# Sums of squares on TensorE and single-tile weight folds at the start of a hybrid encoder block

## The chip, the cores and the metric

The kernel runs on one core of a Trainium2 chip. The metric is the device time of one execution in microseconds, median of the runs. The engines named below are TensorE (PE, with its weight loads as PEld), VectorE (DVE), ScalarE (ACT), GpSimd (POOL) and SyncE (SP), whose queue issues most DMAs.

## The reference

One layer over x of 2048 positions and 1024 channels, all in float32.

```python
u = rms_norm(x, norm_in_g)                     # x * rsqrt(mean(x*x) + 1e-6) * g
proj = einsum('bsd,de->bse', u, w_in)          # 1024 -> 4096
pool_x, pool_z, m_x, m_z = split(proj, 4)      # 1024 columns each
y_pool = pool_mixer(pool_x, pool_w, pool_scale) * silu(pool_z)   # windows 2, 4, 8, 16; 256x256 per group
y_m = mlstm_branch(m_x, ...) * silu(m_z)       # 4 heads of 256, both directions, chunks of 128
h = x + einsum('bse,ed->bsd', concat(y_pool, y_m), w_out)
return rms_norm(h, norm_out_g)
```

## The kernel before

The input projection is done in two halves of 1024 positions. A half is held as 16 tiles `xs[t, kt]` of 128 channels by 512 positions (t: which 512 positions, kt: which 128 of the 1024 channels). The projection's columns are taken in 16 units of 256, and each unit is one step of Strassen's scheme: seven products P1 to P7 instead of eight, each of 12 matmuls with 512 columns (three per channel block: both operands are split into a high part in fp32r and the rest, `bh`, `bl`, `ah`, `al`). One product is one slot: slots 0 to 6 are the first unit, in the order P1, P2, P5, P6, P7, P3, P4, and slot 7 is P1 of the second unit.

PE, DVE, ACT and POOL run in the order in which the program writes their instructions (a hand-written schedule); DMAs on SP are outside that order. Work that is not part of a product is tied to slots by `at_slot(slot, where, ...)`: "pre" stands ahead of the product, "end" behind it. A slot runs like this: `begin_a` (POOL, sums of weights for the slot four later), `read_banks` (ACT or DVE empty the banks of the product before), `low_a` and `high_a` (weight splits for slots ahead), the "pre" events, the product, the "end" events.

The start of the first half has two side tasks, and the change concerns both.

The norm. `squares(t, kt)` squares a tile on ACT, and DVE adds it to `rn[t]`. `norm_sums` adds over the 128 channels with four one-column matmuls (`rhs=ones[:, 0:1]`), DVE scales, POOL takes the power -1/2. `norm_spread` puts the factors across the partitions with four matmuls against the identity, and ACT copies them to `rn[t]`. Then `scale_x` scales each tile on DVE, `sum_b` forms a product's differences on DVE, `high_b` casts four tiles on ACT, and `low_b` subtracts on DVE. While PE waits, `busy(8)` gives it matmuls whose result nobody reads, and 28 such warm-up matmuls (`warm`) stand at the very start. The second half's norm, much later, uses the same `squares` and `norm_sums`; that stays.

The fold. `pool_w` is multiplied into the first quarter of `w_in`: 16 pieces of two tiles, a tile being two float32 matmuls of 256 columns (each is two instructions on PE) into a PSUM buffer `hw` of a pool of three, a copy on ACT (L295) into one of three buffers `st`, and a DMA to `wp_s`. `fold()` is a generator; `fold_steps(n)` takes n steps of it. Loads go out three pieces ahead. Float32 matmuls show as two instructions each, so the four matmuls of `norm_sums` are eight.

Of the kernel before, what the change touches and what calls it, by code (L numbers as in the profile page):

```python
# [10 lines left out]
F32 = mybir.dt.float32  # L11
F32R = mybir.dt.float32r
AF = mybir.ActivationFunctionType
ALU = mybir.AluOpType
# [3 lines left out]
P = 128  # L18
S = 2048
D = 1024  # L20
KT = D // P
NB = 4
BT = S // NB
# [4 lines left out]
EPS = 1e-6  # L28
# [25 lines left out]
def hymba_block(ctx, tc, xT, x, w_in, wpxT, pool_w, bqT, bkT, bvT, bv, w_g, b_g, par, edge, w_out, g_out, out):  # L54
    nc = tc.nc

    def open_pool(stack, name, bufs=1, side="left", **kw):
        return stack.enter_context(tc.tile_pool(name=name, bufs=bufs, side=side, reuse_waits="tile", **kw))
# [4 lines left out]
    wp_s = dram.tile([8, P, KT, P], F32, name="wp_s")  # L63
# [14 lines left out]
    ones = cpool.tile([P, P], F32, name="ones")  # L78
# [10 lines left out]
    ob = open_pool(ctx, "ob", bufs=4)  # L89
# [23 lines left out]
    psp = open_pool(ph1, "psp", side="right", space=PSUM)  # L113
    bstack = {k: ExitStack() for k in reversed(PRODUCTS)}
    bpool = {k: open_pool(stack, f"b{k}", side="right") for k, stack in bstack.items()}
    B, A, raw, sums = {}, {}, {}, {}
# [78 lines left out]
    xs, rn, rs, xq = {}, {}, {}, {}  # L195

    def load_x(pool, p, t):
        for kt in range(KT):
            xs[t, kt] = pool.tile([P, BT], F32, name=f"x{t}{kt}")
            nc.sync.dma_start(out=xs[t, kt], in_=xT[2 * p + t][:, kt, :])  # L200

    def squares(t, kt):
        sq = ob.tile([P, BT], F32, name="op")
        nc.scalar.activation(sq, xs[t, kt], AF.Square)
        if kt == 0:
            rn[t] = xq[t].tile([P, BT], F32, name=f"rn{t}")
            nc.vector.tensor_copy(rn[t], sq)
        else:
            nc.vector.tensor_tensor(rn[t], rn[t], sq, op=ALU.add)

    def norm_sums(pool, t):
        ss = psg.tile([P, 512], F32, name="pg")
        for i in range(4):
            nc.tensor.matmul(ss[:, i:i + 1], lhsT=rn[t][:, i * P:(i + 1) * P], rhs=ones[:, 0:1], start=True, stop=True)
        rs[t] = pool.tile([P, 4], F32, name=f"rs{t}")
        nc.vector.tensor_scalar(rs[t], ss[:, 0:4], 1.0 / D, EPS, op0=ALU.mult, op1=ALU.add)
        nc.gpsimd.tensor_tensor(rs[t], rs[t], mhalf, op=ALU.pow)

    def norm_spread(t):
        rb = psg.tile([P, BT], F32, name="pg")  # L220
        for i in range(4):
            nc.tensor.matmul(rb[:, i * P:(i + 1) * P], lhsT=rs[t][:, i:i + 1].to_broadcast([P, P]), rhs=ident,
                             start=True, stop=True)
        nc.scalar.copy(rn[t], rb)

    def scale_x(t, kt):
        nc.vector.scalar_tensor_tensor(xs[t, kt], in0=xs[t, kt], scalar=par_sb[:, kt, 9:10], in1=rn[t], op0=ALU.mult,
                                       op1=ALU.mult)
# [18 lines left out]
    def low_b(k):  # L247
        hi, lo = B[k]
        for q in range(4):
            nc.vector.tensor_tensor(lo[:, q], block(k, q), hi[:, q].bitcast(F32), op=ALU.subtract)  # L250
# [8 lines left out]
    def unit(U):  # L259
        return PLANS[U // UNITS][U % UNITS]  # L260
# [4 lines left out]
    psk = open_pool(pmp, "psk", bufs=3, space=PSUM)  # L265
# [4 lines left out]
    AHEAD = 3  # L270

    def fold():
        pws, wts = {}, {}
        pieces = [(g, kt) for g in range(4) for kt in range(0, KT, 2)]

        def load(g, kt):
            if kt == 0:
                pws[g] = fop.tile([P, 2, HD], F32, name="pw", bufs=2)
                nc.sync.dma_start(out=pws[g], in_=pool_w[g])
            wts[g, kt] = fop.tile([P, 2, 2 * P], F32, name="wt", bufs=AHEAD + 1)  # L280
            nc.sync.dma_start(out=wts[g, kt], in_=wpxT[g][:, :, kt * P:(kt + 2) * P])

        for t in range(-AHEAD, len(pieces)):
            if t + AHEAD < len(pieces):
                load(*pieces[t + AHEAD])
            if t >= 0:
                g, kt = pieces[t]
                wt, pw = wts.pop((g, kt)), pws[g]
                for e in range(2):
                    ps = psk.tile([P, 2, P], F32, name="hw")  # L290
                    for ct in range(2):
                        nc.tensor.matmul(ps, lhsT=wt[:, ct, e * P:(e + 1) * P], rhs=pw[:, ct, :], start=(ct == 0),  # L292
                                         stop=(ct == 1))
                    st = fop.tile([P, 2, P], F32, name="st", bufs=3)
                    nc.scalar.copy(st, ps)  # L295
                    nc.sync.dma_start(out=wp_s[2 * g:2 * g + 2, :, kt + e, :].rearrange("c p n -> p c n"), in_=st)
            yield

    mvs, mxs, cs, small, toks = {}, {}, {}, {}, {}
# [321 lines left out]
    def at_slot(g, where, what, *args):  # L621
        events.setdefault((g, where), []).append(lambda: what(*args))
# [11 lines left out]
    def order(U):  # L634

        return ("P1", "P2", "P5", "P6", "P7", "P3", "P4") if U == 0 else PRODUCTS


    def weights_of(g, what, *ks):
        U, k = divmod(g, SLOTS)  # L640
        if U < 2 * UNITS:
            k = order(U)[k]
            if not ks or k in ks:
                what(unit(U), k)

    def begin_a(g):
        weights_of(g, sum_a, "P5", "P6", "P7", "P3")
# [35 lines left out]
    def open_x(t):  # L683
        left["x", t] = ExitStack()
        xq[t] = open_pool(left["x", t], f"xq{t}")

    def fold_steps(n):
        for _ in range(n):
            next(folds, None)
# [18 lines left out]
    for p, plan in enumerate(PLANS):  # L708
# [16 lines left out]
        g = G + BEGIN[p][-1] + 7  # L725
# [34 lines left out]
    V, G = nc.vector, nc.gpsimd  # L760
# [15 lines left out]
    fop = open_pool(fos, "fop", side="right")  # L776
# [59 lines left out]
    at_slot(2 * E0 - LAST - 1, "top", open_back)  # L836

    warm = psg.tile([P, 512], F32, name="pg")
    for i in range(28):
        nc.tensor.matmul(warm[:, :P], lhsT=ones, rhs=ones, start=True, stop=True)  # L840
    schedule = tc.manual_schedule(engines={ENG.PE, ENG.DVE, ENG.Activation, ENG.Pool})
    with schedule:
        open_x(0)
        open_x(1)
        load_x(xq[0], 0, 0)
        load_raw(unit(0))
        load_x(xq[1], 0, 1)
        fold_steps(AHEAD)

        def busy(n):  # L850
            idle = psk.tile([P, 2, P], F32, name="hw")
            for i in range(n):
                nc.tensor.matmul(idle[:, 0, :], lhsT=ones, rhs=ones, start=True, stop=True)

        for kt in range(KT):
            squares(0, kt)
        norm_sums(xq[0], 0)
        busy(8)
        for kt in range(4):
            squares(1, kt)  # L860
        norm_spread(0)
        busy(8)
        for g in range(4):
            begin_a(g)
        weights_of(0, high_a)
        scale_x(0, 0)
        scale_x(0, 1)
        weights_of(0, low_a)
        scale_x(0, 2)
        scale_x(0, 3)  # L870
        high_b("P1")
        low_b("P1")
        for kt in range(4, KT):
            squares(1, kt)
        weights_of(1, high_a)
        for kt in range(4, KT):
            scale_x(0, kt)
        high_b("P2")
        at_slot(0, "end", norm_sums, xq[1], 1)
        at_slot(0, "end", fold_steps, 3)  # L880
        weights_of(1, low_a)
        low_b("P2")
        weights_of(2, high_a)
        for s, what, *args in ((1, norm_spread, 1), *((2, scale_x, 1, kt) for kt in range(4)), (2, sum_b, "P5", V),
                               (2, high_b, "P5"), (2, low_b, "P5"),
                               *((3, scale_x, 1, kt) for kt in range(4, KT)), (3, sum_b, "P6", V), (3, high_b, "P6"),
                               (3, low_b, "P6"), (4, sum_b, "P7", V), (4, high_b, "P7"), (4, low_b, "P7"),
                               (4, high_b, "P3"), (4, low_b, "P3"), (4, sum_b, "P4", V), (4, high_b, "P4"),
                               (4, low_b, "P4")):
            at_slot(s, "pre", what, *args)  # L890
        for s, n in enumerate((2, 3, 1, 1, 2, 2, 2), 1):
            at_slot(s, "end", fold_steps, n)
        at_slot(2, "end", load_raw, unit(1))
        nc.sync.dma_start(out=bg, in_=b_g.partition_broadcast(P))
        nc.gpsimd.tensor_copy(gacc, bg[:, None, :].broadcast_to([P, NC, 16]))
        for g in range(2 * E0 - LAST):
            slot(g)
# [3 lines left out]
    op = go = None  # L901
# [300 lines left out]
    with tc.manual_schedule(engines={ENG.PE, ENG.DVE, ENG.Activation, ENG.Pool}):  # L1202
# [19 lines left out]
    V, G = nc.vector, nc.gpsimd  # L1222
# [10 lines left out]
    pieces = dict(  # L1233
        keys=lambda t: weigh_keys(t["kv"]),
        mask=mask, weigh=weigh, exponentials=exponentials, scores=scores, weigh_scores=weigh_scores,
        numerators=numerators, ratio_0=ratio0, ratio_1=ratio1, forward=forward, skip=skip,
        transposes=transpose_step, join=join, store=store_step)
# [93 lines left out]
```

## Time and profile before

| | |
|---|---|
| Median of 3 runs | 1514.14 us (1513.15 to 1514.29) |
| Profiled execution | 1513.62 us, span 1511.9 us |
| PE busy | 1444.7 us, 96% of the span |
| DVE busy | 1016.4 us, 67% |
| ACT busy | 681.2 us, 45% |
| POOL busy | 468.1 us, 31% |
| Mean granted clock of PE | 0.981 |

The span is the time from the first to the last instruction in the profile; the execution's own time also has what lies around it. Matmuls overlap, so a busy PE is not PE at its peak; the time from one start to the next tells more than a duration. The granted clock is given as a share of 2.4 GHz.

### The profile page before, as it was taken

The page shows a single profiled execution, that of the slowest core. Times are in us where ns is not written, and L with a number is a line of the kernel's source. Part 1 is how long each engine was busy: PE and PEld are TensorE (multiplying, and loading weights), DVE is VectorE, ACT ScalarE, POOL GpSimd, SP SyncE. Part 2 cuts the span into 40 slices and gives each one's busy share as a digit, 9 for nine tenths or more (in the row PEclk, how much of TensorE's full clock was granted, in tenths as well). Part 3 has the DMA queues.
Part 4 walks back from the last instruction along what each step waited for, and adds up shares of the span by engine and source line. Part 5 has one row for each costly group of instructions (what it writes and reads, how often), then busy time and mean ns, then how long its engine had stood idle before and what let it go on. Part 6 is the DMA issues. An engine that isn't in the chain of part 4 may idle for free.

```text
span 1511.9 us, 21506 instructions
## 1 busy us (share of the span) xinstructions
PE 1444.7 (96%) x6811; PEld 1206.7 (80%) x6811; DVE 1016.4 (67%) x1990; ACT 681.2 (45%) x1566; POOL 468.1 (31%) x635
## 2 busy tenths in 40 slices
PE   7799999999889999998989798999999999999998
PEld 6688888887767888887767687888888888888886
DVE  6655556779995656778986475667777777666553
ACT  5455555443464555653344433334443445433321
POOL 2113334545461224355430222232333323121100
PEclk8999999999999999999999999999999999999999
DMA  5564544532223544452236878877777767665442
GB/s 211 167 170 152 168 147 136 175 144 75 97 71 108 172 149 159 147 167 67 70 103 197 248 227 257 238 214 226 209 233 226 211 195 214 196 198 150 135 136 84
DMA packets 259345, 251.34 MB, mean 166 GB/s; under 512 B 19744, under 2 KB 219680, under 8 KB 259232
## 3 DMA queue, kind: packets, MB, share of 16 engines
q1 hardware_dynamic: 258080, 247.87, 53.9%
q10 hardware_dynamic: 1152, 2.10, 0.5%
q8 instruction: 54, 0.88, 0.3%
q14 instruction: 59, 0.48, 0.1%
HBM read 168.30 MB, written 81.60 MB: 165 GB/s over the span
## 4 chain that ended last, share of the span: by engine, by line
PE 76%; DVE 10%; DMA 7%; issue 3%; ACT 2%; POOL 1%; SPq 1%; ACTq 0%; DVEq 0%; POOLq 0%
PE po L959 21%; PE psy L175 17%; PE psz L175 8%; PE num L1091 6%; PE upd L800 6%; PE hw L373 4%; PE psx L175 4%; PE num L1086 3%; DVE al L151 2%; DMA ym_s<-yt 2%; PE sT L1076 2%; DVE blP L250 1%; PE hw L292 1%; PE py L1143 1%; DVE win L473 1%
## 5 line engine op out<-in xcount | busy, mean ns | idle before, releaser
L175 PE MATMUL psy<-bhP,ah 128*128 128x512 f32 x512 | 212.7, 415 | 19.8 <-ACT bhP L244 8.3
L959 PE MATMUL po<-woh,yh 128*128 128x512 f32 x512 | 218.2, 426 | 0.7 <-ACT yh L96 0.7
L175 PE MATMUL psy<-blP,ah 128*128 128x512 f32 x512 | 203.2, 397 | 2.5 <-DVE blP L250 2.5
L175 PE MATMUL psy<-bhP,al 128*128 128x512 f32 x512 | 203.9, 398 | 1.1 <-DVE al L151 1.1
L959 PE MATMUL po<-woh,yl 128*128 128x512 f32 x512 | 202.0, 395 | 0.0
L959 PE MATMUL po<-wol,yh 128*128 128x512 f32 x512 | 201.7, 394 | 0.0
L800 PE MATMUL upd<-v,kw 128*128 128x258 f32 x480 | 125.5, 384 | 9.2 <-ACT kw L794 4.7
L175 PEld LDWEIGHTS psy<-bhP,ah 128*128 128x128 f32 x512 | 98.5, 192 | 42.7 <-issue 11.3
L151 DVE TENSOR_TENSOR al<-w,ah 128x512 fp32r<-128x512 f32 x96 | 92.1, 959 | 59.4 <-ACT ah L145 56.1
L1149 ACT ACTIVATE yt<-cT,par_sb 128x128 f32<-128x128 f32 x128 | 44.5, 394 | 186.8 <-DMA ym_s<-yt 186.8
L1065 POOL TENSOR_TENSOR cw<-cT,gw 128x512 f32<-128x512 f32 (+1 forms) x64 | 78.5, 1226 | 161.1 <-issue 72.9
L151 DVE TENSOR_TENSOR al<-sum,ah 128x512 fp32r<-128x512 f32 x128 | 95.3, 757 | 42.6 <-ACT ah L145 42.6
L350 DVE SCALAR_TENSOR_TENSOR c<-mx,par_sb,c 128x384 f32<-128x384 f32 (+1 forms) x160 | 117.8, 736 | 6.2 <-ACT c L345 1.9
L175 PEld LDWEIGHTS psy<-bhP,al 128*128 128x128 f32 x512 | 97.8, 191 | 23.3 <-DVE al L151 1.9
L175 PEld LDWEIGHTS psy<-blP,ah 128*128 128x128 f32 x512 | 98.3, 192 | 22.1 <-DVE blP L250 3.4
L959 PEld LDWEIGHTS po<-woh,yl 128*128 128x128 f32 x512 | 96.5, 188 | 22.3 <-DVE yl L99 0.2
L959 PEld LDWEIGHTS po<-woh,yh 128*128 128x128 f32 x512 | 96.7, 189 | 20.2 <-ACT yh L96 1.1
L376 POOL TENSOR_TENSOR gacc<-gacc,tokst 128x48 f32<-128x48 f32 (+1 forms) x80 | 32.2, 402 | 259.6 <-ACT tokst L374 257.0
L959 PEld LDWEIGHTS po<-wol,yh 128*128 128x128 f32 x512 | 96.9, 189 | 19.3
L175 PE MATMUL psz<-bhP,ah 128*128 128x512 f32 x256 | 106.3, 415 | 2.0 <-ACT bhP L244 2.0
L800 PEld LDWEIGHTS upd<-v,kw 128*128 128x128 f32 x480 | 87.0, 190 | 23.3 <-ACT kw L794 5.8
L145 ACT CAST ah<-sum 128x512 fp32r<-128x512 f32 x128 | 79.6, 623 | 53.0 <-PE psy L175 29.1
(219 smaller groups left out, 3126.2 us busy)
## 6 DMA issues: line engine op xcount, KB each, us to landing
w<-in_w_in SPq DMA_DIRECT2D x48, 512.0 KB, 3.7
gw<-g_s SPq DMA_DIRECT2D x128, 128.0 KB, 5.4
v<-v_s SPq DMA_DIRECT2D x124, 129.0 KB, 4.6
kk<-kk_s SPq DMA_DIRECT2D x124, 128.0 KB, 4.6
x<-in_xT SPq DMA_DIRECT2D x32, 256.0 KB, 6.0
sz_s<-op SPq DMA_DIRECT2D x32, 256.0 KB, 2.8
w<-wp_s SPq DMA_DIRECT2D x16, 512.0 KB, 3.6
y<-yp_s SPq DMA_DIRECT2D x16, 512.0 KB, 5.5
```

The costliest lines, as they stand in the source:

```text
L145: nc.scalar.copy(hi, v)
L151: nc.vector.tensor_tensor(lo, v, hi.bitcast(F32), op=ALU.subtract)
L175: pe(nc.tensor.matmul(ps, lhsT=l[:, q, :], rhs=r[:, q, :], start=(first and q == 0 and n == 0), stop=(q == 3 and n == 2), skip_group_check ...
L350: nc.vector.scalar_tensor_tensor(c[:, :m], in0=mx[:, o + t:o + t + m], scalar=par_sb[:, i, t:t + 1], in1=c[:, :m], op0=ALU.mult, op1=ALU.add)
L373: nc.tensor.matmul(ps[:, e, :], lhsT=src[:, o:o + P], rhs=mvs[i][:, v], start=True, stop=True)
L376: nc.gpsimd.tensor_tensor(gb, gb, st[:, :n, :16], op=ALU.add)
L800: pe(nc.tensor.matmul(ps[:, m, :E], lhsT=t["kw"][:, ms], rhs=t["v"], start=True, stop=True))
L959: pe(nc.tensor.matmul(ps, lhsT=l[:, kt, :], rhs=r, start=(kt == 0 and e == 0), stop=(kt == 7 and e == 2)))
L1065: eng.tensor_tensor(a["cw"][:, ds], a["cT"][:, None].broadcast_to([P, nd, 2, P]), a["gw"][:, 1, ds, None, :].broadcast_to([P, nd, 2, P]), ...
L1086: pe(nc.tensor.matmul(num[:, d, :E], lhsT=a["dd"][:, d, :], rhs=a["kv"]["v"], start=True, stop=d not in a["dirs"]))
L1091: pe(nc.tensor.matmul(num[:, d, :E], lhsT=a["cw"][:, d, m, :], rhs=state[:, m, :], start=False, stop=(m == 1)))
L1149: nc.scalar.activation(a["yt"][:, m, :], a["cT"][:, m, :], AF.Copy, scale=par_sb[:, i, 8:9])
```

## The change

The first half's squares are no longer added by DVE. `squares_on_pe` squares on ACT and lets PE add over the channels at once: four one-column matmuls per tile, into four PSUM banks that stay open over the eight tiles; `norm_factors` then reads the four banks with four small DVE operations. The last four tiles of the second 512 positions, which stood behind P1's operands, now stand ahead of the first `scale_x`. Both `busy(8)` go, and 16 warm-up matmuls stand instead of 28. `fold()` now makes one tile a step, and a step first copies and stores the tile three steps back; three steps are given to most slots' ends, and nine stand in the "pre" part of slots 2, 3 and 4.

```diff
+    def norm_factors(pool, t, parts):
         rs[t] = pool.tile([P, 4], F32, name=f"rs{t}")
-        nc.vector.tensor_scalar(rs[t], ss[:, 0:4], 1.0 / D, EPS, op0=ALU.mult, op1=ALU.add)
+        n = 4 // len(parts)
+        for i, part in enumerate(parts):
+            nc.vector.tensor_scalar(rs[t][:, i * n:(i + 1) * n], part, 1.0 / D, EPS, op0=ALU.mult, op1=ALU.add)
         nc.gpsimd.tensor_tensor(rs[t], rs[t], mhalf, op=ALU.pow)
+    def squares_on_pe(t, kt):
+        sq = ob.tile([P, BT], F32, name="op")
+        nc.scalar.activation(sq, xs[t, kt], AF.Square)
+        if kt == 0:
+            sums[t] = [psk.tile([P, 2, P], F32, name="hw")[:, 0] for i in range(2)]
+            sums[t] += [psp.tile([P, BT], F32, name=f"ps{c}") for c in "xz"]
+        for i, ss in enumerate(sums[t]):
+            nc.tensor.matmul(ss[:, 0:1], lhsT=sq[:, i * P:(i + 1) * P], rhs=ones[:, 0:1], start=(kt == 0),
+                             stop=(kt == KT - 1))
+        if kt == KT - 1:
+            rn[t] = xq[t].tile([P, BT], F32, name=f"rn{t}")
+            norm_factors(xq[t], t, [ss[:, 0:1] for ss in sums.pop(t)])
...
+        tiles = [(g, kt, n) for g, kt in pieces for n in range(2)]
+        def store(t):
+            g, kt, n = tiles[t]
+            st = fop.tile([P, 2, P], F32, name="st", bufs=3)
+            nc.scalar.copy(st, banks_.pop(t))
+            nc.sync.dma_start(out=wp_s[2 * g:2 * g + 2, :, kt + n, :].rearrange("c p n -> p c n"), in_=st)
+        for p in pieces[:AHEAD]:
+            load(*p)
+        yield
+        for t in range(len(tiles) + 3):
+            if t >= 3:
+                store(t - 3)
+            if t < len(tiles):
+                g, kt, n = tiles[t]
+                if n == 0 and t // 2 + AHEAD < len(pieces):
+                    load(*pieces[t // 2 + AHEAD])
+                wt, pw = wts[g, kt], pws[g]
+                ps = banks_[t] = psk.tile([P, 2, P], F32, name="hw")
+                for ct in range(2):
+                    nc.tensor.matmul(ps, lhsT=wt[:, ct, n * P:(n + 1) * P], rhs=pw[:, ct, :], start=(ct == 0),
+                                     stop=(ct == 1))
             yield
...
-    for i in range(28):
+    for i in range(16):
         nc.tensor.matmul(warm[:, :P], lhsT=ones, rhs=ones, start=True, stop=True)
...
-        fold_steps(AHEAD)
-        for kt in range(KT):
-            squares(0, kt)
-        norm_sums(xq[0], 0)
-        busy(8)
+        fold_steps(1)
         for kt in range(KT):
+            squares_on_pe(0, kt)
         for kt in range(4):
-            squares(1, kt)
+            squares_on_pe(1, kt)
         norm_spread(0)
-        busy(8)
         for g in range(4):
             begin_a(g)
         weights_of(0, high_a)
+        for kt in range(4, KT):
+            squares_on_pe(1, kt)
         scale_x(0, 0)
...
         low_b("P1")
-        for kt in range(4, KT):
-            squares(1, kt)
         weights_of(1, high_a)
...
-        at_slot(0, "end", norm_sums, xq[1], 1)
         at_slot(0, "end", fold_steps, 3)
...
-                               (2, high_b, "P5"), (2, low_b, "P5"),
+                               (2, high_b, "P5"), (2, fold_steps, 3), (2, low_b, "P5"),
                                *((3, scale_x, 1, kt) for kt in range(4, KT)), (3, sum_b, "P6", V), (3, high_b, "P6"),
-                               (3, low_b, "P6"), (4, sum_b, "P7", V), (4, high_b, "P7"), (4, low_b, "P7"),
+                               (3, fold_steps, 3), (3, low_b, "P6"), (4, sum_b, "P7", V), (4, high_b, "P7"),
+                               (4, fold_steps, 2), (4, low_b, "P7"),
                                (4, high_b, "P3"), (4, low_b, "P3"), (4, sum_b, "P4", V), (4, high_b, "P4"),
-                               (4, low_b, "P4")):
+                               (4, fold_steps, 1), (4, low_b, "P4")):
             at_slot(s, "pre", what, *args)
-        for s, n in enumerate((2, 3, 1, 1, 2, 2, 2), 1):
+        for s, n in enumerate((3, 3, 3, 3, 3, 3, 40), 1):
             at_slot(s, "end", fold_steps, n)
```

## Rows read from the trace of the kernel before

**Rows 1.** The page's first part: busy us (share of the span) and instructions, whole span

```profile
PE 1444.7 (96%) x6811; PEld 1206.7 (80%) x6811; DVE 1016.4 (67%) x1990; ACT 681.2 (45%) x1566; POOL 468.1 (31%) x635
```

**Rows 2.** Stretches: us; busy of PE, PEld, DVE, ACT, POOL; granted clock; DMA; GB/s

```profile
1.20:6.60 5.40, 5.40 (x25) 5.40 (x26) 0.43 (x1) 1.94 (x3) 0.18 (x1) 1.00 0.63 187
6.70:10.20 3.50, 3.50 (x32) 3.38 (x31) 2.17 (x4) 2.10 (x5) 0.00 (x0) 1.00 0.98 354
10.30:13.30 3.00, 0.00 (x0) 0.00 (x0) 2.58 (x4) 1.69 (x3) 0.00 (x0) 1.00 1.02 401
13.50:16.90 3.40, 3.40 (x17) 3.40 (x17) 1.09 (x3) 1.75 (x3) 1.58 (x2) 0.50 1.05 392
16.90:20.30 3.40, 3.40 (x18) 3.40 (x17) 3.19 (x3) 0.78 (x2) 2.28 (x2) 0.50 1.09 372
...
47.40:50.10 2.70, 0.51 (x2) 0.19 (x1) 2.27 (x5) 2.11 (x5) 0.00 (x0) 1.00 0.90 232
51.10:54.40 3.30, 3.30 (x10) 2.53 (x9) 3.30 (x6) 0.00 (x0) 0.00 (x0) 0.50 0.25 84
59.80:63.60 3.80, 0.50 (x1) 0.19 (x1) 0.71 (x2) 3.23 (x8) 0.00 (x0) 1.00 0.57 174
64.70:68.00 3.30, 3.30 (x9) 2.61 (x8) 3.30 (x7) 0.00 (x0) 0.00 (x0) 0.50 0.57 144
69.70:72.50 2.80, 0.56 (x2) 0.19 (x1) 0.74 (x2) 2.67 (x6) 0.00 (x0) 1.00 0.56 160
100.00:160.00 60.00, 60.00 (x313) 51.15 (x312) 31.83 (x46) 35.73 (x79) 17.88 (x26) 1.00 0.55 166
```

**Rows 3.** Order of time, first 60 us: start, us, engine, line, out<-in, shape, count, idle before

```profile
13.30 1.65 PEld L214 LDWEIGHTS pg<-ones,rn 128*128 128x128 f32 x8 [3.23 <-issue]
...
18.45 1.91 PE L222 MATMUL pg<-ident,rs 128*128 128x128 f32 x8
...
25.02 0.50 PE L175 MATMUL psy<-blP,ah 128*128 128x512 f32 x1 [2.04 <-DVE blP L250]
```

**Rows 4.** Order of time on PE, 394 to 400 us: the second half's norm sums

```profile
396.50 1.02 PE L214 MATMUL pg<-ones,rn 128*128 128x1 f32 x8 [2.44 <-DVE rn L209]
397.38 0.48 PE L175 MATMUL psy<-bhP,ah 128*128 128x512 f32 x1
```

**Rows 5.** Order of time on ACT, start and operands of P5

```profile
11.71 0.63 ACT L204 ACTIVATE op<-x 128x512 f32<-128x512 f32 x1 [0.34 <-DMA x<-in_xT]
15.05 2.67 ACT L204 ACTIVATE op<-x 128x512 f32<-128x512 f32 x4 [2.71 <-DMA x<-in_xT]
20.40 0.59 ACT L224 COPY rn<-pg 128x512 f32<-128x512 f32 x1 [2.68 <-PE pg L222]
...
48.77 2.18 ACT L244 CAST bhP<-x 128x512 fp32r<-128x512 f32 x4
```

**Rows 6.** Order of time on DVE: scaling, adds of squares, differences

```profile
21.02 1.42 DVE L227 SCALAR_TENSOR_TENSOR x<-x,par_sb,rn 128x512 f32<-128x512 f32 x2 [0.42 <-DMA bg<-in_b_g]
...
26.69 3.95 DVE L209 TENSOR_TENSOR rn<-rn,op 128x512 f32<-128x512 f32 x4
...
46.51 2.48 DVE L238 TENSOR_TENSOR x<-x,x 128x512 f32<-128x512 f32 x4
```

**Rows 7.** Groups on ACT, 20 to 97 us: busy, mean ns, idle before, what ended it

```profile
L295 ACT COPY st<-hw 128x256 f32<-128x256 f32 x30 | 11.0, 375 | 31.2 <-DMA wp_s<-st 14.5 <-issue 9.1 <-PE hw L292 7.5
```

**Rows 8.** Chain of waits that ended last, 20 to 98 us: start, us, what

```profile
50.17 0.26 PE psz L175
...
72.51 2.78 PE psy L175 x11
...
85.94 3.45 PE hw L292 x16
89.39 2.73 PE psy L175 x12
...
97.30 0.93 PE psz L175 x4
```

More of the change, by code (lines that the diff above doesn't have):

```diff
@@ L214, in norm_sums @@
             nc.tensor.matmul(ss[:, i:i + 1], lhsT=rn[t][:, i * P:(i + 1) * P], rhs=ones[:, 0:1], start=True, stop=True)
+        norm_factors(pool, t, [ss[:, 0:4]])
+    def norm_factors(pool, t, parts):
         rs[t] = pool.tile([P, 4], F32, name=f"rs{t}")
-        nc.vector.tensor_scalar(rs[t], ss[:, 0:4], 1.0 / D, EPS, op0=ALU.mult, op1=ALU.add)
+        n = 4 // len(parts)
+        for i, part in enumerate(parts):
+            nc.vector.tensor_scalar(rs[t][:, i * n:(i + 1) * n], part, 1.0 / D, EPS, op0=ALU.mult, op1=ALU.add)
         nc.gpsimd.tensor_tensor(rs[t], rs[t], mhalf, op=ALU.pow)
+    def squares_on_pe(t, kt):
[10 more added lines that the diff above has]
+            norm_factors(xq[t], t, [ss[:, 0:1] for ss in sums.pop(t)])
     def norm_spread(t):
@@ L281, in load @@
             nc.sync.dma_start(out=wts[g, kt], in_=wpxT[g][:, :, kt * P:(kt + 2) * P])
[L283 to L296, printed above, removed]
+        tiles = [(g, kt, n) for g, kt in pieces for n in range(2)]
+        banks_ = {}
+        def store(t):
[18 more added lines that the diff above has]
+                                     stop=(ct == 1))
             yield
@@ L847, in hymba_block @@
         load_x(xq[1], 0, 1)
-        fold_steps(AHEAD)
[L850 to L853, printed above, removed]
+        fold_steps(1)
         for kt in range(KT):
-            squares(0, kt)
-        norm_sums(xq[0], 0)
-        busy(8)
+            squares_on_pe(0, kt)
         for kt in range(4):
-            squares(1, kt)
+            squares_on_pe(1, kt)
         norm_spread(0)
-        busy(8)
         for g in range(4):
```

## The prediction

> **What bounds the kernel now.** The page's first part says it: TensorE (PE) is busy for 96% of the span, the next engine for 67% [rows 1]. From 100 us on PE is busy without a break at the full granted clock [rows 2]. The order of instructions from there on is the same in both kernels and PE takes them back to back, so what the first 97 us gain or lose reaches the end one for one. The rest is read in that start alone: first the busy time by stretches, with the granted clock; then the order of time for PE, ACT and DVE; then the chain of waits.
>
> The stretches show two things. PE stands idle or nearly so several times (10.3 to 13.3, 47.4 to 50.1, 59.8 to 63.6), and after each the clock is at 0.50, the lower of its two levels (1.2 of 2.4 GHz), for a stretch (13.5 to 20.3, 51.1 to 54.4, 64.7 to 68.0) [rows 2]. In the first 6.6 us the column still reads 1.00, but the rate of instructions there is half that of 6.7 to 10.2, so that stretch I count as half clock too. What brings it back differs: 3.3 us of dense 512-column products do at 54.4 and at 68.0, but the 3.4 us from 13.5 to 16.9, as fully busy, do not. That stretch began with the eight one-column instructions of the norm sums (L214); only the next, all of 128 columns, ended with the clock up [rows 2, 3].
>
> PE waits for the chain squares, sum, spread, scale, cast, low part. The first scaling starts at 21.02 [rows 6], the first product runs from 25.02 [rows 3], P5 from 50.17, P7 from 72.51, and the point at which all 32 fold tiles have passed PE is 97.30 [rows 8] (the second unit's P5 starts there). ACT loses 31.2 us ahead of 30 fold copies, because a copy waits for its tile on PE or for the store that frees its buffer, and the casts of the next product queue behind it [rows 7].
>
> **The change part by part, in its new order.** I follow each engine's queue as the program writes it.
>
> *Warm-up and first squares.* 32 instructions remain of 56. 25 of them take 5.4 us, the other 7 run at 3.5 us for 32 [rows 2]: PE is free at about 7.4 instead of 10.3. The sums of the first half need 8 groups, each of 4 matmuls, which are 8 instructions of one column. The trace shows such a group: 0.88 us from its start to the next instruction's at full clock (396.50 to 397.38) [rows 4], and 1.65 us of weight loads at half clock (13.30) [rows 3]. Which price holds decides the case. Before, the clock was down at 13.5 after PE had stood idle from 10.3. The stretch that began with one-column work did not bring it back at 16.9, so I take such work not to hold it either, and let the clock fall as soon after the end of the wide work as then: full clock for 3 groups of 0.88, to about 10.0, then half. Five groups at 1.65 end at 18.3 (at full clock 14.4). ACT's squares are no limit: the last is done at 11.71 + 0.63 = 12.34 [rows 5].
>
> The Trainium skill, "TensorE: Matmul & The Clock Gate", Part 1, has the clock follow how busy PE has recently been, and its section on LDWEIGHTS prices a load of 128 columns at about 107 ns without regard to the clock. By that page PE, which has no gap in this stretch, would keep 0.86 us a group, and the sum would be that of the rival "clock held" below; the rows of 13.3 to 16.9 speak against it.
>
> *Next squares and the spread.* The second half's first four tiles are squared by 17.72 [rows 5]. Their banks need DVE's four small reads (about 0.5 us), so PE starts them at 18.8: 4 x 1.65 gives 25.4. norm_spread is queued behind them: 1.91 us [rows 3], 27.3; ACT's copy, 0.2 + 0.59 [rows 5], 28.1 (before: 20.99).
>
> *The last four squares, moved ahead of the scaling.* This is the dear part. ACT casts one weight block (0.63, as a square) and squares tile 4: 29.3. PE adds four groups: 35.9. DVE's four reads for the second half now stand ahead of the first scaling in DVE's queue: 36.4, against 21.02, so +15.4. From scaling to P1's steady run took 4.0 us (21.02 to 25.02) and takes that again: 40.5. P1 itself is mostly at half clock: ends at 44.8.
>
> *What comes back.* DVE's adds are gone (3.95 us at 26.69 [rows 6] lay between P1's and P2's operands, the rest of them earlier), and only 3 fold tiles stand between P1 and P2, not 6. A tile is a quarter of 3.45 us, 0.86; a product 2.73 [rows 8]. Three tiles: 47.4; the second spread at full clock, 0.96 (half of 1.91): 48.3; P2 to 51.1; three tiles: 53.7.
>
> *Folds ahead of P5, P6, P7.* A tile needs the bank of the tile three before, and that tile's copy stands on ACT behind the casts of the product. So these tiles do not fill PE's wait for the casts, they start when it is over, and the product is queued behind them. For P5: second-half scaling (4 x 0.71) from 50.5, differences 2.48 [rows 6], last cast 56.4, first copy 56.8; three tiles, at half clock for most of it after PE's 3 us of idling, 4.2 us: P5 from 61.0 (before 50.17 [rows 8], with 10 tiles done, now 9). P5 and three tiles: 66.4. P6's casts wait for ACT's copy of P5's bank and take 2.18 [rows 5]: 67.4; copy and three tiles: 70.4; P6 and three tiles: 75.7. P7: casts end 76.6, two tiles 78.7; but one more tile is queued behind the casts for P4, which need DVE's low part of P3 and its differences for P4, operations of one shape, 2.48 each [rows 6]: DVE 80.4, 82.9, casts 83.5, copy 83.9, tile at half clock 85.6. P7 is queued behind it and ends, partly at half clock, at 89.7. Before, those DVE steps lay beside P7. The copies themselves cost nothing: stores are three tiles old, and ACT's lost 31.2 us mostly go; but what then ends last is DVE.
>
> *Tail.* PE no longer waits: 11 tiles 9.5, P3, P4 and the next unit's P1 8.2, its maps 0.5: 107.9 at the point that was 97.30. **Sum +10.6 us.** SP's loads move little: each fold load still goes out three pieces ahead.
>
> The profiled execution took 1513.6 (span 1511.9), 0.5 under the median. 1513.6 + 10.6 = 1524.2, given as 1524. Where the clock falls again (57 to 61, 82 to 88 in this sum) is chance; without those falls about 3 us less, with the first fall later about 2 less, and 1.91 for the spread and 4.2 for the tiles are upper ends: the likeliest case alone is 1519 to 1527.
>
> **Rivals.**
>
> *Clock held.* One-column work keeps full clock (no row shows it held by that alone; the stretch at 13.5 is a rise that failed, not a fall). Then the first half's sums end at 14.4, the next four groups (from 15.7) at 19.4, spread and copy at 21.1, the last groups at 25.8, scaling at 26.4: still +5.4, since the reordering remains. P2 then comes 3 us earlier than before with 3 tiles owed, P5 at 51, P6 at 60.4, P7 only at 75.9 because of the fold behind P4's casts. At 97.30's place: 98. Result 1514 to 1517.
>
> *The fold pipeline fills the gaps: faster.* Clock held, and the tiles ahead of P5, P6 and P7 run inside PE's waits. Their idle parts at 47.4, 59.8 and 69.7 are 2.2, 3.3 and 2.2 us, and the half-clock stretches at 51.1 and 64.7 cost half of 3.3 each [rows 2]. 7.7 + 3.3, less the 5.4 of the later scaling, is 5.6 faster: 1508.5. It decides if the copies do not wait for the casts, that is, if the first tile of each group starts before the product's first cast. Against it: the copies are written behind the casts and ACT's casts are seen to queue behind copies in the same way [rows 7]. Full clock throughout with the copies where they are written would still give back only 2 to 3 us, within 0.2%.
>
> *The change does not do what it says.* The adds leave DVE in any case; but the copies may still wait for stores (three buffers as before), so ACT's 31.2 us would stay and P6 come no earlier relative to P5: 3 to 4 us on top, 1527 to 1528.
>
> **Chances.** Likeliest case 0.64, clock held 0.18, gaps filled 0.10, copies still waiting 0.08. A measurement here tells 0.2% (3.0 us) from no change. Slower 0.71: the first and the last, less a little; same 0.18; faster 0.11. To hold 8 in 10 the range takes in clock held and most of the last: 1513 to 1528; what lies below is the faster rival, and above only the worst of the last.
>
> **What would show it.** Right: in the changed profile the granted clock is 0.50 from about 10 to beyond 40 us; a group of one-column matmuls takes about 1.65 us; DVE's first scaling stands near 36, P1's run near 40; PE waits longest ahead of P7, for ACT's copy of a fold tile behind P4's casts; ACT's waits ahead of its fold copies for stores are a few us in all; from 110 us on everything matches, shifted. Wrong: first scaling near 26 (clock held); a fold tile between P5's cast and the end of the fold before it (gaps filled); PE's order not that of the program.

## The result, and the profile after

The changed kernel takes 1530.84 us (median of 6 runs, 1525.56 to 1533.01), the kernel before 1513.7 in the same runs (6, 1512.48 to 1514.63): a ratio of 1.0108, 95% interval 1.0093 to 1.0122; by the medians it is 17.1 us slower. Forecast were 1524 us and a range up to 1528. The direction and the mechanism held; the size was too small by 6 to 7 us, and the range ended 3 us too early.

The profiled execution took 1530.16 us, its span is 1528.5, against 1513.62 and 1511.9 before; the mean granted clock is 0.971 against 0.981. The page's first part, busy us with shares and instructions:

```profile
PE 1460.4 (96%) x6867; PEld 1222.0 (80%) x6867; DVE 1009.2 (66%) x1980; ACT 681.7 (45%) x1566; POOL 467.1 (31%) x635
```

Beside [rows 1] PE has 15.7 us more of busy time for 56 instructions more. Most of that is PE at half clock: `wide_sums` below, which has as many instructions and kept the clock until 29.6 us, has 1448.8 us, 4.1 more than before. The stretches of the changed kernel (us; busy of PE, PEld, DVE, ACT, POOL; granted clock; DMA; GB/s):

```profile
6.40:11.50 5.10, 5.10 (x48) 5.08 (x46) 0.00 (x0) 3.68 (x7) 0.00 (x0) 1.00 0.97 361
6.40:24.40 18.00, 18.00 (x107) 17.77 (x105) 0.63 (x4) 6.46 (x11) 3.53 (x3) 0.64 1.01 359
11.60:42.20 30.60, 24.37 (x102) 22.71 (x102) 10.08 (x21) 10.08 (x18) 7.35 (x6) 0.50 0.47 166
...
55.90:62.70 6.80, 5.88 (x14) 4.71 (x15) 6.80 (x12) 2.47 (x7) 0.00 (x0) 0.50 0.38 105
83.30:90.00 6.70, 5.27 (x12) 4.16 (x13) 2.86 (x5) 2.30 (x6) 2.27 (x3) 0.50 0.44 115
110.00:160.00 50.00, 50.00 (x258) 42.45 (x257) 26.07 (x36) 29.27 (x63) 15.22 (x22) 1.00 0.49 150
...
412.40:423.00 10.60, 10.60 (x40) 8.45 (x40) 7.94 (x10) 2.89 (x6) 6.37 (x4) 0.75 0.21 56
```

The second and third lines are the case. From 6.4 to 24.4 us PE is busy without a gap, and within that time, at 11.55, the clock falls (0.64 is the mean over this time). From 11.6 to 42.2 us it is at the lower one, while PE is busy for 24.37 of 30.60 us. Before, the first such stretch ran from 13.5 to 20.3 [rows 2]. From 110 to 160 us PE is full at full clock, as it was before from 100 to 160.

The order of time of all engines in the start (start, us, engine, line, out<-in, shape, count, idle before) shows what happens in it:

```profile
7.29 0.53 PEld L232 LDWEIGHTS hw<-ones,op 128*128 128x128 f32 x4
8.18 0.53 PEld L232 LDWEIGHTS hw<-ones,op 128*128 128x128 f32 x4
...
12.12 0.97 PEld L232 LDWEIGHTS hw<-ones,op 128*128 128x128 f32 x4
13.83 0.97 PEld L232 LDWEIGHTS hw<-ones,op 128*128 128x128 f32 x4
...
22.43 2.05 PE L241 MATMUL pg<-ident,rs 128*128 128x128 f32 x8
25.52 2.19 ACT L227 ACTIVATE op<-x 128x512 f32<-128x512 f32 x4
31.95 0.16 DVE L221 TENSOR_SCALAR rs<-hw 128x1 f32<-128x1 f32 x1 [16.02 <-PE hw L232]
33.34 1.42 DVE L246 SCALAR_TENSOR_TENSOR x<-x,par_sb,rn 128x512 f32<-128x512 f32 x2
38.49 0.80 PE L175 MATMUL psy<-blP,ah 128*128 128x512 f32 x1 [2.90 <-DVE blP L269]
```

A group of the one-column sums (L232) takes 0.89 us from one start to the next at full clock (7.29 to 8.18) and 1.71 at half (12.12 to 13.83). ACT squares its last four tiles by 27.7, but DVE stands idle for 16.02 us until PE has added them up at 31.95: the four small reads are queued ahead of the first scaling, which starts at 33.34, against 21.02 in [rows 6]. P1 runs from 38.49, against 25.02 in [rows 3].

PE's own order of time further on:

```profile
56.81 5.49 PE L325 MATMUL hw<-pw,wt 128*128 128x256 f32 x12 [4.96 <-ACT st L308]
...
78.07 1.99 PE L325 MATMUL hw<-pw,wt 128*128 128x256 f32 x8 [0.95 <-ACT st L308]
84.73 2.07 PE L325 MATMUL hw<-pw,wt 128*128 128x256 f32 x4 [4.66 <-ACT st L308]
86.24 0.99 PE L175 MATMUL psy<-bhP,ah 128*128 128x512 f32 x1
...
108.57 1.99 PE L325 MATMUL hw<-pw,wt 128*128 128x256 f32 x8 [0.78 <-ACT st L308]
110.22 0.59 PE L175 MATMUL psz<-bhP,ah 128*128 128x512 f32 x1
...
410.76 1.70 PE L214 MATMUL pg<-ones,rn 128*128 128x1 f32 x8 [2.44 <-DVE rn L209]
```

Twice PE waits nearly 5 us for ACT's copy of a fold tile (L308): at 56.81 ahead of P5, and at 84.73 for the one tile behind P4's casts; P7 follows at 86.24. The row at 110.22 is the second unit's P5. The chain of [rows 8] has a row of it at 97.30; in PE's order of time before it starts at 96.95, so it is 13.3 us later:

```profile
96.95 0.58 PE L175 MATMUL psz<-bhP,ah 128*128 128x512 f32 x1
```

ACT's fold copies, in the groups of 20 to 112 us (busy, mean ns, idle before, what ended it):

```profile
L308 ACT COPY st<-hw 128x256 f32<-128x256 f32 x32 | 10.9, 380 | 13.4 <-PE hw L325 10.2 <-DMA wp_s<-st 3.0
```

The idle time ahead of them fell from 31.2 us to 13.4, that for stores from 14.5 to 3.0 [rows 7]. This part of the change does what it should; it was not what PE waited for.

### The profile page after: what moved, and what is told of

It reads as the page before. It is cut to its first block, busy times and chain, and to the rows that moved or that the text cites. A ratio compares the mean times of both kernels' runs of the same rounds, so it can differ in the third digit from the quotient of the medians.

```text
span 1528.5 us, 21601 instructions
## 1 busy us (share of the span) xinstructions
PE 1460.4 (96%) x6867; PEld 1222.0 (80%) x6867; DVE 1009.2 (66%) x1980; ACT 681.7 (45%) x1566; POOL 467.1 (31%) x635
## 3 DMA queue, kind: packets, MB, share of 16 engines
q1 hardware_dynamic: 258080, 247.87, 53.3%
## 4 chain that ended last, share of the span: by engine, by line
PE 60%; DVE 8%; DMA 4%; issue 2%; ACT 1%; POOL 1%; SPq 0%; ACTq 0%; DVEq 0%; POOLq 0%
PE po L980 22%; PE psy L175 10%; PE num L1112 6%; PE upd L830 6%; PE psz L175 5%; PE num L1107 3%; PE hw L403 2%; PE psx L175 2%; DVE al L151 2%; PE sT L1097 2%; DMA ym_s<-yt 1%; PE py L1164 1%; DVE blP L269 1%; DVE win L503 1%; POOL sum L138 1%
## 5 line engine op out<-in xcount | busy, mean ns | idle before, releaser
L145 ACT CAST ah<-sum 128x512 fp32r<-128x512 f32 x128 | 79.6, 623 | 60.4 <-PE psy L175 30.7
```

Of the source, the lines that this page charges most:

```text
L145: nc.scalar.copy(hi, v)
```

## The experiments

Each ran beside the kernel before on the same chip, whose median was 1514.8, 1517.25 or 1515.0 there (1513.7 beside the changed kernel's first runs); so ratios are compared. The edits are on the changed kernel where nothing else is said. The diffs here are shortened: of a long line they show only the part that differs. The runs answer three questions: which half of the change costs what, which of its steps costs what, and where the forecast's missing 6 us are.

### The two halves of the change

`squares_alone`: the changed kernel with `fold()` (its body is not shown) and its places as before.

```diff
-        fold_steps(1)
+        fold_steps(AHEAD)
...
-(2, fold_steps, 3), (3, fold_steps, 3), (4, fold_steps, 2), (4, fold_steps, 1)
...
-enumerate((3, 3, 3, 3, 3, 3, 40), 1)
+enumerate((2, 3, 1, 1, 2, 2, 2), 1)
```

> The squares on TensorE, their new place and the shorter warm-up, with the folds as before. If the loss of the whole change (+17 us on the median) comes from the one-column sums and the lost clock, this part alone is 10 to 16 us slower than before, the clock is at 0.50 from about 12 to 42 us, and the first scaling stands near 33 us as in the whole change. If the rival holds, that the fold tiles queued ahead of P5, P6 and P7 are the dear part, it is at most 4 us slower.

Measured: 1529.86 us, ratio 1.0103 (1.0086 to 1.0121). The clock is at 0.50 from 11.3 to 42.0 us and the first scaling starts at 33.55, as in the whole change.

`folds_alone`: the kernel before with the new `fold()` and its places, the diff above the other way round.

> The single-tile folds with their new places, the squares on DVE as before, with both busy calls and 28 warm-up matmuls. If the squares are the dear part: within 3 us of before, since what the late copies give back (ACT's 31 us of waits) is lost again ahead of P7, which must wait for the tile behind P4's casts (P7 near 75 instead of 72). If the fold places are the dear part: 8 to 14 us slower.

Measured: 1517.81, ratio 1.0019 (1.0008 to 1.0030). The squares carry most of the loss; the folds cost about 3 us by themselves.

### The steps that cost

`wide_sums`: the same sums, with 128 equal columns in place of one.

```diff
-nc.tensor.matmul(ss[:, 0:1], lhsT=sq[...], rhs=ones[:, 0:1], start=(kt == 0),
+nc.tensor.matmul(ss[:, 0:P], lhsT=sq[...], rhs=ones, start=(kt == 0),
```

> The whole change, but each sum of squares is a matmul of 128 columns of ones instead of one column (the same sum in every column, the first is read). If one-column work is what loses the clock, the clock stays at 1.00 from the warm-up to P1, a group of four takes about 0.9 us, the first scaling stands near 26 instead of 33, and the whole comes out 7 to 10 us under the change: within 5 us of before. If the clock falls for another reason (the shorter warm-up, PE waiting for ACT), the wider matmuls cost as much or more: 0 to 5 us over the change.

Measured: 1523.38, ratio 1.0049 (1.0035 to 1.0063). Its stretches:

```profile
7.00:26.00 19.00, 15.70 (x136) 15.12 (x135) 0.79 (x6) 9.29 (x16) 3.53 (x3) 1.00 0.98 354
29.60:36.40 6.80, 4.69 (x11) 3.77 (x12) 6.80 (x10) 3.68 (x7) 0.91 (x1) 0.50 0.00 0
```

and DVE's order of time:

```profile
26.56 1.41 DVE L246 SCALAR_TENSOR_TENSOR x<-x,par_sb,rn 128x512 f32<-128x512 f32 x2
```

With 128 columns PE is busy for a smaller share of the time (15.70 of 19.00 us, against 18.00 of 18.00 above), and the clock stays at 1.00 until PE waits for P1's operands. The width of the sums is all that differs, so it was the one-column sums that lost the clock here, and that is worth about 0.6% against the changed kernel's first runs (1.0108). The first scaling starts at 26.56; the rival "clock held" had worked out 26.4 for just this. Half of the loss is left, which that rival had not: it put the whole at 1514 to 1517. From P5 on the start is some 3 us later than its numbers (P5 at 54.22 for 51, P6 at 63.38 for 60.4, the second unit's P5 at 101.29 for 98); the second half's scaling takes 5.80 us here too, which comes up below.

`squares_behind_p1`: the last four tiles' squares behind P1, one-column as in the change.

```diff
-        for kt in range(4, KT):
-            squares_on_pe(1, kt)
...
+        for kt in range(4, KT):
+            at_slot(0, "end", squares_on_pe, 1, kt)
```

> The whole change, but the last four squares of the second 512 positions stand at the end of slot 0, behind P1, instead of ahead of the first scaling. If their place ahead of the scaling costs what it delays, 7 to 8 us come back: first scaling near 25, and the whole 5 to 8 us under the change. If the four groups cost PE the same wherever they stand (6.6 us at half clock, now between P1 and P2), P1 comes 8 us earlier and P2 does not, and the whole is within 2 us of the change.

Measured: 1524.42, ratio 1.0060 (1.0047 to 1.0072). DVE's order of time, then a stretch:

```profile
25.15 1.77 DVE L246 SCALAR_TENSOR_TENSOR x<-x,par_sb,rn 128x512 f32<-128x512 f32 x2 [9.40 <-ACT rn L243]
```

```profile
36.40:46.40 10.00, 10.00 (x40) 9.37 (x40) 2.96 (x8) 2.28 (x5) 2.98 (x3) 0.50 0.00 0
```

The first scaling moves from 33.34 to 25.15, but not all of it is kept: the one-column sums now lie behind P1. PE waits 2.32 us for the first of them, and then the clock is at 0.50 from 36.4 to 46.4 although PE has no gap in it (10.00 of 10.00; sums until 42.9, fold tiles behind them). The rows of PE and of DVE:

```profile
36.19 0.92 PE L232 MATMUL hw<-ones,op 128*128 128x1 f32 x4 [2.32 <-ACT op L227]
...
49.10 2.74 DVE L246 SCALAR_TENSOR_TENSOR x<-x,par_sb,rn 128x512 f32<-128x512 f32 x4 [4.63 <-ACT rn L243]
```

The second row is the second half's scaling for P5, which takes 5.80 us in the changed kernel. Here GpSimd's sums are over at 48.7, before it starts; so a part of what this run gives back comes from there.

`p4_fold_behind`, and `folds_p4_behind` as the same edit on `folds_alone`: the tile that stood behind P4's casts goes to the end of the slot.

```diff
-(4, fold_steps, 1), (4, low_b, "P4")
+(4, low_b, "P4")
...
-enumerate((3, 3, 3, 3, 3, 3, 40), 1)
+enumerate((3, 3, 3, 4, 3, 3, 40), 1)
```

> The whole change with one step of the fold moved: the tile that is queued ahead of P7 behind P4's casts goes to the end of slot 4. If P7's wait for that tile is on the path, P7 starts near 79 instead of 86 and the whole is 3 to 5 us under the change. If DVE's work for P3 and P4, which the wait hid, only comes due later, the whole is within 1 us of the change.

> The kernel before (squares on DVE) with the single-tile folds, and the tile behind P4's casts moved to the end of slot 4. If the late copies give back what ACT lost ahead of its copies, and only the queue ahead of P7 swallowed it, this is 1 to 4 us faster than before, with P7 near 67 to 68 instead of 72. If the fold pipeline gains nothing, it is level with before or up to 3 us slower, as with that tile in place.

Measured: 1527.59, ratio 1.0063 (1.0045 to 1.0082), and 1517.15, ratio 0.9999 (0.9990 to 1.0008). PE's order of time in `folds_alone`, with the tile ahead of P7:

```profile
73.91 2.07 PE L306 MATMUL hw<-pw,wt 128*128 128x256 f32 x4 [4.66 <-ACT st L289]
75.42 0.99 PE L175 MATMUL psy<-bhP,ah 128*128 128x512 f32 x1
```

and in `p4_fold_behind`, without it:

```profile
79.70 1.99 PE L325 MATMUL hw<-pw,wt 128*128 128x256 f32 x8 [0.95 <-ACT st L308]
81.34 0.58 PE L175 MATMUL psy<-bhP,ah 128*128 128x512 f32 x1
```

The wait of 4.66 ahead of P7 is gone; that of 0.95 ahead of the two tiles stood in the changed kernel too (78.07). P7 starts 8.3 us after P6 instead of 14.8 in the changed kernel (71.41 to 86.24); behind P7 PE waits 1.93 us for the next copy. On the kernel before, this one tile is, by the medians, the whole of what the new folds cost. In `folds_p4_behind` P7 starts at 67.90, as was expected for a gain, and the second unit's P5 at 94.81, for 96.95 before; yet the whole is level, so those 2.1 us of the start are not seen at the end.

`no_pre_folds`: no fold tile stands ahead of any product.

```diff
-(2, fold_steps, 3), (3, fold_steps, 3), (4, fold_steps, 2), (4, fold_steps, 1)
...
-enumerate((3, 3, 3, 3, 3, 3, 40), 1)
+enumerate((6, 6, 4, 4, 4, 4, 40), 1)
```

> The whole change with all nine fold steps that stand ahead of products moved to the ends of the two slots before (6, 6, 4, 4, 4, 4 at the ends). If tiles queued ahead of P5, P6 and P7 behind the casts hold those products back, P5 starts near 57, P6 near 66, P7 near 73 to 76, and the whole is 3 to 6 us under the change. If it is only the order in which the same work is done, the whole is within 1.5 us of the change.

Measured: 1523.98, ratio 1.0045 (1.0027 to 1.0062). P5 starts at 58.13, P6 at 67.06 and P7 at 73.46, near what was expected if the tiles hold the products back. With all tiles at the ends about half of the loss goes; the interval overlaps with that of the one tile moved (1.0063), so it is not shown to be more. And a long wait stays in PE's order of time, for the first copy of the tiles that now stand behind P7:

```profile
81.52 5.41 PE L325 MATMUL hw<-pw,wt 128*128 128x256 f32 x16 [4.76 <-ACT st L308]
```

`wide_behind_p4`: `wide_sums`, `squares_behind_p1` and `p4_fold_behind` together.

> The whole change with three parts altered together: sums of 128 columns, the last four squares behind P1, P4's fold at the end of slot 4. If the lost clock, the place of the last squares and the tile ahead of P7 are the three dear parts and add up, 13 to 16 us come back and the whole is within 2.5 us of before. If they overlap (each was one way to the same wait), 9 to 11 us come back, as with the dearest alone or little more, and it stays 4 to 6 us over before.

Measured: 1515.91, ratio 1.0001 (0.9989 to 1.0012). With the three steps undone and all else of the change left in, the loss is gone. Alone they gave back 0.59%, 0.48% and 0.45% against the changed kernel's first runs (1.0108), and 0.46%, 0.35% and 0.32% against its second (1.0095, below): 1.5% or 1.1% together, for a loss of about 1.0%. Each of these ratios is known to about 0.15%, so whether the three simply add up or overlap is not shown.

### Where the missing 6 us are

`sums_off_scaling`: GpSimd's sums of weights are held until the second half's scaling for P5 is over, and the first of them has a buffer of its own. The sums themselves stay.

```diff
-        sums[k] = ap.tile([P, 4, P], F32, name="sum", bufs=3)
+        if k == "P3" and not first_sum:
+            first_sum.append(k)
+            sums[k] = ob.tile([P, BT], F32, name="op").rearrange("p (a b) -> p a b", a=4)
+        else:
+            sums[k] = ap.tile([P, 4, P], F32, name="sum", bufs=3)
...
+        def hold_pool():
+            nc.gpsimd.tensor_copy(held, xs[1, 3][:, 0:1])
...
-(2, high_b, "P5"), (2, fold_steps, 3)
+(2, high_b, "P5"), (2, hold_pool), (2, fold_steps, 3)
```

> The whole change, but GpSimd's sums of weights do not run beside the scaling for P5: the first unit's sum for P3 has a buffer of its own and runs earlier, and the next unit's sums wait for a small copy that reads the last scaled tile. If GpSimd working beside it is why DVE's four scalings took 5.80 us and not 2.8 to 3.8, they take 2.8, the first tile ahead of P5 stands near 54 instead of 56.8, and the whole is 2 to 4 us under the change. If the scaling is slow for another reason, it stays near 5.8 and the whole within 1 us.

Measured: 1528.10, ratio 1.0078 (1.0064 to 1.0092): 2.6 to 4.5 us under the changed kernel's two measurements, as was expected, though its interval overlaps with that of the second. The order of time on DVE and on GpSimd in the changed kernel:

```profile
46.65 2.22 POOL L138 TENSOR_TENSOR sum<-w,sum 128x512 f32<-128x512 f32 x1 [9.37 <-DVE al L151]
48.95 1.60 POOL L138 TENSOR_TENSOR sum<-w 128x512 f32<-128x512 f32 x1
50.63 1.59 POOL L138 TENSOR_TENSOR sum<-sum,w 128x512 f32<-128x512 f32 x1
...
47.63 5.80 DVE L246 SCALAR_TENSOR_TENSOR x<-x,par_sb,rn 128x512 f32<-128x512 f32 x4
53.35 2.48 DVE L257 TENSOR_TENSOR x<-x,x 128x512 f32<-128x512 f32 x4
```

and in `sums_off_scaling`:

```profile
50.11 2.73 DVE L251 SCALAR_TENSOR_TENSOR x<-x,par_sb,rn 128x512 f32<-128x512 f32 x4
58.18 4.80 DVE L251 SCALAR_TENSOR_TENSOR x<-x,par_sb,rn 128x512 f32<-128x512 f32 x4
...
58.26 1.81 POOL L143 TENSOR_TENSOR sum<-w 128x512 f32<-128x512 f32 x1
60.15 1.62 POOL L143 TENSOR_TENSOR sum<-sum,w 128x512 f32<-128x512 f32 x1
```

Four scalings beside three sums take 5.80 us, alone 2.73, and the next four, which then have two sums beside them, 4.80: about 1.0 us for each sum that runs beside them. From P1's steady run to P5 it is 17.8 us here and 23.3 in the changed kernel; 3.1 of the difference are the scaling, and 2.4 the three tiles ahead of P5, which ran at full clock here. The Trainium skill, "SBUF — State Buffer", section "Who interferes with whom", states that a DVE instruction with two inputs in SBUF contends with a GpSimd instruction that reads SBUF. These rows agree: the scaling reads `x` and `rn`, and its time grows by about 1.0 us for each sum beside it. The sum that was moved ahead holds DVE up there instead: P1's low part takes 3.56 us, for 2.48 in the changed kernel.

`shift_only`: the kernel before with 120 dense instructions of 128 columns put into PE's queue at 142 us, whose result nobody reads.

```diff
+        def idle_pe(n):
+            idle = psg.tile([P, 512], F32, name="pg")
+            for i in range(n):
+                nc.tensor.matmul(idle[:, :P], lhsT=ones, rhs=ones, start=True, stop=True)
...
+        at_slot(20, "end", idle_pe, 60)
```

> The kernel before with 60 matmuls of 128 columns at the end of slot 20, whose result nobody reads: 120 instructions at 0.115 us, 13.8 us of dense work on TensorE, long after the start. If a delay in the start reaches the end one for one, the whole is 13.8 us (12.5 to 15) over before. If a later start makes the rest slower (clock falls that before escapes), it is 16 to 19 us over.

Measured: 1529.38, ratio 1.0081 (1.0067 to 1.0095), 12.1 us more. PE's order of time:

```profile
141.98 13.56 PE L858 MATMUL pg<-ones 128*128 128x128 f32 x120
```

A delay of 13.56 us came out as 12.1 (10.2 to 14.4): passed on one for one within the interval, and not made larger. The median lies just under the 12.5 that was expected.

`change_again`: the changed kernel without an edit.

> The changed kernel unaltered, beside before and the next three on one chip, since before itself has differed between chips by up to 3.5 us. If the whole loss is what the start shows (13 us at the point where the folds are done, passed on one for one), it is 11.5 to 14.5 us over before here. If something after 110 us adds to it, it is again 16 to 17 us over.

Measured: 1530.63, ratio 1.0095 (1.0078 to 1.0112), 15.6 us more by the medians. That lies between the two expectations, and the interval reaches into both: it does not decide between them. A stretch of this execution:

```profile
9.60:47.00 37.40, 31.17 (x129) 29.18 (x130) 11.96 (x24) 14.14 (x25) 7.34 (x6) 0.50 0.44 159
```

Here the clock fell at 9.6, not at 11.55, and the first scaling started at 36.26 (forecast 36.4), P1 at 41.41, the second unit's P5 at 111.78. So the point of the first fall differs from one execution to the next by 2 us, and the start by 1.6 to 3.

### A version that combines what helped

`warm42_folds_p4`: `folds_p4_behind` with 42 warm-up matmuls instead of 28, so that PE does not stand idle ahead of the norm sums.

```diff
-    for i in range(28):
+    for i in range(42):
```

> The kernel before with the single-tile folds (P4's tile at the end of slot 4) and 42 warm-up matmuls instead of 28, so that TensorE has wide work until the first norm sums at 13.3. If the idle 3 us from 10.3 are why the clock falls at 13.5 before, it stays at 1.00 until P1's operands are awaited, the spread ends 1.5 to 2.5 us earlier, first scaling near 19, and the whole is 2 to 5 us under before: faster than both kernels. If the clock falls anyway, or DVE and ACT set the pace from there, it is within 1.5 us of before.

Measured: 1513.24, ratio 0.9987 (0.9976 to 0.9997), 1.8 us faster than the kernel before. Its stretches:

```profile
13.40:15.50 2.10, 0.87 (x8) 0.90 (x9) 0.98 (x2) 0.00 (x0) 0.00 (x0) 1.00 1.05 395
15.70:19.00 3.30, 3.30 (x17) 3.30 (x17) 2.22 (x4) 2.53 (x4) 2.98 (x3) 0.50 1.04 376
```

The clock still fell, at 15.6 instead of by 13.5, and was back at 19.0; the first scaling started at 21.13, no earlier than in [rows 6]. The gain is under 0.2%, and in the profiled execution it does not come from the earlier scaling that was expected. The second unit's P5 starts at 94.56, 2.4 us earlier than before, but with 28 warm-up matmuls it had started at 94.81. The interval overlaps with that of `folds_p4_behind` (0.9990 to 1.0008), so it is not shown that the longer warm-up does anything.

## Why the prediction was right in kind and too small

**Held.** The norm sums' one column: the clock fell at 11.55 (forecast about 10.0) and came back only at 42.2, a group took 1.71 us (1.65), and `wide_sums` shows that the clock stays up with 128 columns in the same place. The Trainium skill's "TensorE: Matmul & The Clock Gate", Part 1, has the clock follow how busy PE has been. Going by the busy time of the profile it would have stayed up here: PE was busy for 18.00 of 18.00 us from 6.4 to 24.4, and the clock fell in the middle, as the forecast had it. The last four squares delay the first scaling through DVE's queue: 16.02 us of waiting, 33.34 (36.4). The tile behind P4's casts holds P7: 86.24 (85.6). The tiles ahead of P5 start when ACT's casts are over: 56.81 (56.8). Stores no longer hold ACT: 3.0 us. That 56.81 and 86.24 are met so closely is luck: two errors of 3 us, named below, cancel in this execution; in the second one the same starts are 59.75 and 87.92.

**The rivals.** "Clock held" fell with the rows at 11.6 to 42.2, though its start of the first scaling was borne out by `wide_sums` (26.56 for 26.4); behind that its numbers were 3 us short there as well. "Gaps filled" fell: PE waited 4.96 and 4.66 us for copies written behind the casts. "Copies still waiting for stores" fell with the 3.0 us in the groups.

**The step that failed: "second-half scaling (4 x 0.71)".** The sum took the price of one scaling from 21.02 in [rows 6], where GpSimd was idle. It took 5.80 us, not 2.84, since three of GpSimd's sums fell beside it (`sums_off_scaling`: 2.73 without them); 5.38 in the second execution. The kernel before had shown this price too, in two rows that the sum did not use, DVE's and GpSimd's order of time:

```profile
42.83 3.75 DVE L227 SCALAR_TENSOR_TENSOR x<-x,par_sb,rn 128x512 f32<-128x512 f32 x4
...
43.05 1.67 POOL L138 TENSOR_TENSOR sum<-sum,w 128x512 f32<-128x512 f32 x1 [2.00 <-issue]
```

One sum beside four scalings there, and 1.0 us more. A delay that moves an engine's work beside other work has to be priced at the new place. Up to this scaling the start ran about 3 us ahead of the sum (33.34 for 36.4, 47.63 for 50.5), because PE came to the first sums at 6.40 and not 7.4 and the clock fell at 11.55 and not about 10.0; behind the scaling it was level with the sum (53.4 for 53.3). In the second execution, with the fall where the sum had put it, nothing made up for it: its P5 started at 63.72, for 61.0.

**Also too small.** The three tiles ahead of P5 took 4.9 us (56.81 to 61.74), for 4.2, which the forecast had called an upper end: the clock was at 0.50 from 55.9 to 62.7, all the way. From P5 to P7 it was 24.5 us, as in the sum (24.6); but from P7 to the end point, with the tail of 11 tiles, P3, P4 and P1, it was 24.0 (86.24 to 110.22), for 22.3. Three terms make up this difference. P7 was at half clock for most of its run and took 4.7 (4.1). A product takes 2.96 from its start to that of what follows it, not 2.73, the length of a row of the chain in [rows 8]. And "PE no longer waits" did not hold: the second unit's maps with the wait behind them (0.78, the row at 108.57) took 1.5, for 0.5. The tiles took 8.9, for 9.5. At the end point the loss was 13.3 us in one execution and 14.8 in the other, for 10.6 (10.9 counted from 96.95).

**"Passed on one for one."** `shift_only` bears it out for a pure delay. Yet from the second unit's P5 to the end of the span it is 1414.9 us in the profile before (1511.9 less 96.95) and 1418.3 after (1528.5 less 110.22), and the code there is the same. Over the profiles of these runs this stretch lies between 1413.0 (`wide_behind_p4`) and 1420.9 (`p4_fold_behind`), `shift_only` aside, which has its delay in it. The forecast's premise, that PE is busy at full clock from 100 us on, rested on a row that ends at 160 us; later PE waits and the clock falls, in both kernels. Added up from the granted clock in the traces, PE is at 0.50 in this stretch for 37.5 us before and for 45.8 after. The 8.3 us more cost at most half of that, 4.1, and the stretch is 3.3 longer.

At 410.76 one of these falls can be seen: the second half's norm sums wait the same 2.44 us as in [rows 4], but in the changed kernel the clock falls with them (0.75 is the mean over 412.4 to 423.0). Before, it did not, over the same work:

```profile
398.10:408.70 10.60, 8.68 (x42) 6.99 (x42) 9.16 (x12) 3.71 (x7) 6.38 (x4) 1.00 0.25 66
```

The change is not needed for it: in `folds_alone`, `folds_p4_behind`, `warm42_folds_p4` and `shift_only`, which have the norm of the kernel before, the clock falls at these sums too, and in `p4_fold_behind`, which has that of the changed kernel, it does not. So the last 3.3 us of the 16.6 between the two spans are falls of the clock that executions of the same code have or do not have, and the profile before lay near the short end. The median of the kernel before beside the changed kernel, 1513.7, was at the low end too, with 1514.8 to 1517.25 in the other groups of runs, and beside `change_again` the loss was 15.6 us and not 17.1. What decides where the clock falls in this stretch stays open.

The range was too narrow by these terms: it held bounds for the clock and for the tiles, but none for the scaling, and none for the spread of the rest.

## What to carry to other kernels

Before small work is moved onto a busy engine, look at what it does to the clock of the work around it: here sums of one column on TensorE cost 7 to 9 us by the clock (`wide_sums`), and even with the clock kept (`wide_behind_p4`) taking the adds off VectorE gained nothing that can be measured. A tile that is to fill a wait must not itself depend on what ends the wait: the tile queued behind P4's casts held P7 up by 4.66 us, and behind P7 it did not. Take the price of an operation from a row in which its neighbours are those that it will have at the new place.

## What the runs showed of the hardware

With PE busy without a gap by the profile, the clock can fall and can stay at its lower level: it fell at 11.55 us in the changed kernel, within one-column sums that kept PE busy for 18.00 of 18.00 us, and in `squares_behind_p1` it was at 0.50 from 36.4 to 46.4, with one-column sums and then fold tiles, behind a wait of 2.32 us. The same groups of sums with 128 columns kept 1.00 from 7.0 to 26.0 us and took 0.9 us each, no longer than one-column groups at full clock (0.89). A sum on GpSimd beside DVE's scaling costs DVE about 1.0 us (2.73 alone, 3.75, 4.80 and 5.80 beside one, two and three). Two executions of the same start differed by 2 us in when the clock fell (11.55 and 9.6), and the later part, with the same code, took 1413.0 to 1420.9 us.
